# Eight experts in sequence on one core: two results instead of one go into buffers of earlier results, and both leave by SyncE and ScalarE

## The chip, the cores and the metric

The kernel runs on one core of one Trainium2 chip. The metric is the device time of one execution in microseconds (us). Four executions of the kernel before gave 183.13, 183.03, 182.60 and 182.73 us, a median of 182.88 us. Lower is better.

## The reference: what is computed

Eight experts each apply a two-layer network to their own 256 rows of input. All inputs and outputs are float32.

```python
n_experts, capacity, hidden, expert_hidden = 8, 256, 512, 2048
h = np.matmul(x, w1) + b1[:, np.newaxis, :]      # (8,256,512) @ (8,512,2048)
h = np.maximum(h, 0)
return (np.matmul(h, w2) + b2[:, np.newaxis, :]).astype(np.float32)   # @ (8,2048,512)
```

Each expert has 4 MB of `w1` and 4 MB of `w2`, 512 KB of `x` and 512 KB of result. The profile counts 71.39 MB read from device memory and 4.19 MB written to it.

## The kernel before, in words

The weights are read once, as float32, and turned into float16 on the way by DMAs that GpSimd issues. Everything that GpSimd issues, loads and stores, is written by hand into one list, called `ring` (lines 214 to 225), and stays in that order (`ordered`). The main loop (lines 227 to 234) has stages s = 0 to 10. A stage first puts out the entries of the ring that are due, then computes the first product of expert s (`first_product`: 64 matrix multiplications into PSUM, and ReLU with bias on ScalarE) and the second product of expert s - 3 (`second_product`: the bias row and 32 matrix multiplications into two PSUM tiles `po0` and `po1`). The lag of three stages is `LAG`.

The entries of the ring are, in order, the loads of x, w1 and w2, the second weights of expert 7 in three pieces (8, 4 and 4 sixteenths; `load_w2_piece`), and after all loads the stores: `flush(0)`, `flush(1)` and so on, `flush(e)` being due in stage e + 4 (line 225). So the stores of results 0 to 3 are put out in stage 7, right behind the last load, and those of results 4, 5 and 6 in stages 8, 9 and 10.

GpSimd's DMAs use eight completion semaphores in turn. A DMA is therefore issued only when the one eight places before it has landed. This paces the stores: in the trace each `out_dram<-out` issue on POOL ends a wait for the landing of a piece of weights.

`store(e, po)` (lines 139 to 154) brings a result from PSUM to SBUF: VectorE copies the half `po[0]` (L145), ScalarE the half `po[1]` (L146). The result tile is 128 partitions of 4 KB; partition p holds rows 2p and 2p + 1. For results 0 to 6 the tile comes from `out_pool`, which has seven buffers. Two of the seven first hold the float32 x of experts 0 and 1 (`x32`) and become results 5 and 6. Result 7 has no buffer of its own: it is written into that of result 4 (`REUSED = 4`), so its copies must wait until the store of result 4 has landed. Its store is issued by SyncE (L149).

Result 5 is stored in three pieces (`PARTS`, line 37): partitions 0 to 24 by SyncE as soon as the copies are done (L153), partitions 25 to 120 and 121 to 127 by GpSimd when `flush(5)` is due (L137). All other stores are whole, by GpSimd. In what follows, store e is the store of result e.

Of the kernel before, what the change touches and what calls it, by code (L numbers as in the profile page):

```python
# [11 lines left out]
def kernel(  # L12
# [9 lines left out]
    nc = tc.nc  # L22
    fp32 = mybir.dt.float32
    fp16 = mybir.dt.float16
    E, T, H = x.shape
    M = w1.shape[2]
    P = 128
# [1 line left out]
    nKC = H // P  # L29
    nJ = M // P  # L30
    LAG = 3
    LATE = range(E - 1)
    REUSED = 4

    PARTS = {5: ((0, 25, True), (25, 121, False), (121, 128, False))}
    nXF32 = 2

    def ordered(ins):  # L40
        return tc.keep_in_program_order(ins)
# [5 lines left out]
    x_pool = ctx.enter_context(tc.tile_pool(name="xp", bufs=4))  # L47
    xT_pool = ctx.enter_context(tc.tile_pool(name="xTp", bufs=2))
    hT_pool = ctx.enter_context(tc.tile_pool(name="hT", bufs=LAG + 1))
    out_pool = ctx.enter_context(tc.tile_pool(name="outp", bufs=E - 1))  # L50
    psum_x = ctx.enter_context(tc.tile_pool(name="psum_x", bufs=1, space=bass.MemoryType.PSUM))
    psum_h = ctx.enter_context(tc.tile_pool(name="psum_h", bufs=3, space=bass.MemoryType.PSUM))
    psum_o = ctx.enter_context(tc.tile_pool(name="psum_o", bufs=2, space=bass.MemoryType.PSUM))
# [13 lines left out]
    results = []  # L67
    pending = {}
# [63 lines left out]

    def flush(e):
        dst, src = pending.pop(e)
        for p0, p1, sync in PARTS.get(e, ((0, P, False),)):
            if not sync:
                ordered(nc.gpsimd.dma_start(out=dst[p0:p1], in_=src[p0:p1]))  # L137

    def store(e, po):


        if e < E - 1:
            results.append(out_pool.tile([P, nTB, H], fp32, tag="out", name="out"))
        out_sb = results[e] if e < E - 1 else results[REUSED]
        nc.vector.tensor_copy(out=out_sb[:, 0, :], in_=po[0])  # L145
        nc.scalar.copy(out=out_sb[:, 1, :], in_=po[1])  # L146
        dst = out[e].rearrange("(p tb) h -> p tb h", tb=nTB)
        if e == E - 1:
            nc.sync.dma_start(out=dst, in_=out_sb)  # L149
            return  # L150
        for p0, p1, sync in PARTS.get(e, ()):
            if sync:
                nc.sync.dma_start(out=dst[p0:p1], in_=out_sb[p0:p1])  # L153
        pending[e] = (dst, out_sb)

    def second_product(e):
        po = []
        for tb in range(nTB):
            t = psum_o.tile([P, H], fp32, tag=f"po{tb}", name=f"po{tb}")
            po.append(t)  # L160
            ordered(nc.tensor.matmul(  # L161
                out=t, lhsT=ones1, rhs=b2_sb[0:1, e * H : (e + 1) * H], start=True, stop=False,
            ))
        for lo, hi, t in w2_sb[e]:
            for tb in range(nTB):
                for j in range(lo, hi):
                    ordered(nc.tensor.matmul(  # L167
                        out=po[tb],
                        lhsT=hT[e][:, j, tb * P : (tb + 1) * P],
                        rhs=t[:, j - lo, :],  # L170
                        start=False,
                        stop=(j == nJ - 1),
                    ))
        store(e, po)

    x32 = []
    for e in range(nXF32):
        x32.append(out_pool.tile([P, nTB, H], fp32, tag="out", name="x32"))
        (nc.sync if e == 0 else nc.scalar).dma_start(
            out=x32[e], max_dma_last_dim=2048, in_=x[e].rearrange("(p tb) h -> p tb h", tb=nTB)  # L180
# [4 lines left out]
        out=b2_sb,  # L185
        in_=b2.rearrange("e h -> (e h)").rearrange("(o f) -> o f", o=1),
# [10 lines left out]
    for j in range(nJ):  # L197
        for s in range(2):
            ordered(nc.tensor.matmul(  # L199
                out=pb[s * 64 : (s + 1) * 64, j, :, :],  # L200
# [5 lines left out]
    for s in range(2):  # L206
        nc.vector.tensor_copy(  # L207
            out=b1T[s * 64 : (s + 1) * 64, :, :], in_=pb[s * 64 : (s + 1) * 64, :, :, s]
# [13 lines left out]
    for lo, hi in ((0, 8), (8, 12), (12, 16)):  # L222
        ring.append((0, load_w2_piece, (E - 1, lo, hi)))
    for e in LATE:
        ring.append((e + LAG + 1, flush, (e,)))
# [40 lines left out]
```

## Time and profile before

| what | value | where it is from |
|---|---|---|
| median of four executions | 182.88 us | the times |
| the profiled execution's own time | 183.13 us | the times |
| its span in the trace | 181.3 us | the page |
| outside the span | 1.8 us | 183.13 - 181.3 |
| granted TensorE clock, mean | 0.924 | the times |
| TensorE busy | 135.2 us, 75% | the page, part 1 |
| software DMA queue (GpSimd's) | 38.71 MB, 96.9% of 16 engines' span | the page, part 3 |
| SyncE's queue | 1.15 MB, 1.7% | the page, part 3 |
| ScalarE's queue | 0.59 MB, 1.1% | the page, part 3 |
| stores by GpSimd, 512 KB | 6, median 21.1 us from issue to landing | the page, part 6 |
| store 7 by SyncE, 512 KB | 3.2 us from issue to landing | the DMA view |

The bytes of the queues are counted as they are written, so a weight that arrives as float32 and is kept as float16 counts half. The line of DMA shares in the page gives the mean busy share of the 16 DMA engines in 40 slices of 4.5 us; a 9 means 90% or more. The share in a window can come out a little above 1, since packets of one engine overlap at their ends. In a line of the timeline the bracket gives the idle time of that engine before the instruction and what ended it.

### The profile page before, as it was taken

The numbers are of one execution on the slowest core, as the hardware profiler recorded it, in microseconds if no ns is written. First come the engines' busy times: TensorE is split into PE (matmuls) and PEld (weight loads), VectorE is DVE, ScalarE is ACT, GpSimd is POOL, SyncE is SP. The second block draws the span as 40 slices with busy tenths as digits, with TensorE's granted clock in tenths as the row PEclk, the third lists the DMA queues.
The fourth block names the chain that finished last, engine by engine and source line by source line (L and its number), as shares of the span: only waits on it lengthen the run. The fifth ranks groups of instructions, "written<-read, shape, count | busy, mean of one in ns | idle before, by whom it ended". The sixth has DMA issues, their size and how long they took to land.

```text
span 181.3 us, 2122 instructions
## 1 busy us (share of the span) xinstructions
PE 135.2 (75%) x912; PEld 94.3 (52%) x912; DVE 13.1 (7%) x21; ACT 62.5 (34%) x137; POOL 20.1 (11%) x43
## 2 busy tenths in 40 slices
PE   1725989579650999939990899939998999988900
PEld 1614879459550754936480664936497434333300
DVE  0320011001000101010100101010100101010010
ACT  0021769638670340825081250726078010101010
POOL 7200020300300010201010000200050111111200
PEclk9999999969995589999999589999999999999975
DMA  5999999999999999899989999999999999999994
GB/s 159 264 228 233 220 184 232 194 229 213 233 228 184 224 231 228 181 227 231 224 181 227 232 213 195 231 228 210 199 231 201 211 222 208 224 220 209 358 412 192
DMA packets 5543, 40.58 MB, mean 224 GB/s; under 512 B 638, under 2 KB 654, under 8 KB 3230
## 3 DMA queue, kind: packets, MB, share of 16 engines
q0 software_dynamic: 4784, 38.71, 96.9%
q1 hardware_dynamic: 446, 1.15, 1.7%
q10 hardware_dynamic: 304, 0.59, 1.1%
q8 instruction: 7, 0.11, 0.2%
q14 instruction: 2, 0.02, 0.0%
HBM read 71.39 MB, written 4.19 MB: 417 GB/s over the span
## 4 chain that ended last, share of the span: by engine, by line
DMA 75%; PE 19%; issue 1%; POOL 1%; DVE 0%; POOLq 0%; DVEq 0%
DMA x<-in_x_dram 44%; DMA w2sb<-in_w_dram 15%; PE ph L116 10%; DMA out_dram<-out 9%; DMA w1sb<-in_w_dram 8%; PE po L167 8%; PE psx L103 1%; POOL w2sb L88 1%; PE po L161 1%; DVE out L145 0%; POOL w1sb L78 0%; DVEq L145 0%; POOLq L137 0%; POOLq L250 0%
## 5 line engine op out<-in xcount | busy, mean ns | idle before, releaser
L116 PE MATMUL ph<-xT,w1sb 128*128 128x256 f16 x512 | 67.0, 296 | 10.9 <-DMA w1sb<-in_w_dram 10.9
L123 ACT ACTIVATE hT<-ph,b1T 128x256 f16<-128x256 f32 x128 | 56.9, 473 | 42.0 <-PE ph L116 41.9
L116 PEld LDWEIGHTS <-w1sb 128*128 128x128 f16 x512 | 60.8, 148 | 16.4 <-DMA w1sb<-in_w_dram 11.9
L167 PE MATMUL po<-w2sb,hT 128*128 128x512 f16 x224 | 49.7, 379 | 1.3 <-DMA w2sb<-in_w_dram 1.3
L167 PEld LDWEIGHTS <-hT 128*128 128x128 f16 x256 | 24.5, 98 | 34.0 <-issue 5.8
L146 ACT COPY out<-po 128x512 f32<-128x512 f32 x8 | 4.7, 591 | 62.9 <-PE po L167 50.8
L103 PE MATMUL psx<-ident,x 128*128 128x128 f16 x64 | 6.2, 254 | 19.7 <-DMA x<-in_x_dram 17.9
L103 PEld LDWEIGHTS <-x 128*128 128x128 f16 x64 | 5.0, 124 | 20.7 <-DMA x<-in_x_dram 18.9
L78 POOL DMA_DIRECT2D w1sb<-in_w_dram x8 | 4.5, 558 | 65.2 <-PE ph L116 64.3
L109 DVE COPY xT<-psx 128x1024 f16<-128x1024 f16 x8 | 5.5, 691 | 81.8 <-PE psx L103 81.8
L145 DVE COPY out<-po 128x512 f32<-128x512 f32 x8 | 5.5, 692 | 74.7 <-PE po L167 61.1
L88 POOL DMA_DIRECT2D w2sb<-in_w_dram x9 | 4.8, 535 | 53.7 <-PE po L167 53.7
L137 POOL DMA_DIRECT2D out_dram<-out x8 | 4.3, 532 | 31.3 <-DMA w2sb<-in_w_dram 23.0
L167 PE MATMUL po<-w,hT 128*128 128x512 f16 x32 | 7.1, 379 | 0.8 <-DMA w<-in_w_dram 0.8
L199 PE MATMUL pb<-ident,b_rows 16*64 16x16 f32 x64 | 3.7, 266 | 4.1 <-DMA b_rows<-in_b_dram 4.1
L199 PEld LDWEIGHTS pb<-ident,b_rows 16*64 16x64 f32 x64 | 3.6, 198 | 4.0 <-POOL ident masks.py:199 4.0
L161 PE MATMUL po<-b_sb,ones 1*128 1x512 f16 x16 | 4.8, 379 | 0.0
L123 ACT ACT_TABLE_LOAD x1 | 1.3, 1283 | 9.5 <-DVE b1T L207 9.5
L72 POOL DMA_DIRECT2D x<-in_x_dram x6 | 3.6, 604 | 0.5 <-DMA w1sb<-in_w_dram 0.5
L161 PEld LDWEIGHTS <-ones 1*128 1x128 f16 x16 | 0.9, 92 | 2.1 <-issue 2.1
L194 DVE CAST x<-x 128x1024 f16<-128x1024 f32 x2 | 1.4, 694 | 6.6 <-DMA x<-in_x_dram 6.6
L94 POOL DMA_DIRECT2D w<-in_w_dram x3 | 1.6, 557 | 0.0
(9 smaller groups left out, 2.6 us busy)
## 6 DMA issues: line engine op xcount, KB each, us to landing
w1sb<-in_w_dram POOLq DMA_DIRECT2D x8, 2048.0 KB, 33.8
w2sb<-in_w_dram POOLq DMA_DIRECT2D x5, 2048.0 KB, 46.4
w2sb<-in_w_dram POOLq DMA_DIRECT2D x4, 1024.0 KB, 28.7
out_dram<-out POOLq DMA_DIRECT2D x6, 512.0 KB, 21.1
x<-in_x_dram POOLq DMA_DIRECT2D x6, 256.0 KB, 39.2
w<-in_w_dram POOLq DMA_DIRECT2D x1, 1024.0 KB, 31.1
w<-in_w_dram POOLq DMA_DIRECT2D x2, 512.0 KB, 34.1
x<-in_x_dram SPq DMA_DIRECT2D x1, 512.0 KB, 4.2
```

Of the source, the lines that this page charges most:

```text
L78: ordered(nc.gpsimd.dma_start(out=w1_sb[e], in_=w1[e].rearrange("(p kc) m -> p kc m", kc=nKC)))
L88: ordered(nc.gpsimd.dma_start(out=t[:, lo : lo + step, :], in_=src[:, lo : lo + step, :]))
L103: ordered(nc.tensor.transpose(out=pt[:, kc, tb * P : (tb + 1) * P], in_=x16[e][:, tb, :].rearrange("p (q kc) -> p q kc", kc=nKC)[:, :, kc] ...
L109: nc.vector.tensor_copy(out=xT[e], in_=pt)
L116: ordered(nc.tensor.matmul(out=ph, lhsT=w1_sb[e][:, kc, :].rearrange("p (q j) -> p q j", j=nJ)[:, :, j], rhs=xT[e][:, kc, :], start=(kc == 0),
L123: nc.scalar.activation(out=hT[e][:, j, :], in_=ph, func=mybir.ActivationFunctionType.Relu, bias=b1T[:, j, e : e + 1], scale=1.0,)
L137: ordered(nc.gpsimd.dma_start(out=dst[p0:p1], in_=src[p0:p1]))
L145: nc.vector.tensor_copy(out=out_sb[:, 0, :], in_=po[0])
L146: nc.scalar.copy(out=out_sb[:, 1, :], in_=po[1])
L161: ordered(nc.tensor.matmul(out=t, lhsT=ones1, rhs=b2_sb[0:1, e * H : (e + 1) * H], start=True, stop=False,))
L167: ordered(nc.tensor.matmul(out=po[tb], lhsT=hT[e][:, j, tb * P : (tb + 1) * P], rhs=t[:, j - lo, :], start=False, stop=(j == nJ - 1),))
L199: ordered(nc.tensor.matmul(out=pb[s * 64 : (s + 1) * 64, j, :, :], lhsT=b1_rows.rearrange("r (q j) -> r q j", j=nJ)[:, :, j], rhs=ident[0 ...
```

## The change

Result 6 no longer has a buffer of its own: it is written into the buffer of result 2, and result 7 into that of result 3 instead of result 4. The pool has six buffers instead of seven; results 4 and 5 now take the two that first held x32. GpSimd stores results 0 to 5, each whole, in the ring; results 6 and 7 are stored outside the ring, at once after their copies. Store 7 is whole, by SyncE. Store 6 is cut as store 5 was: partitions 0 to 24 by SyncE, 25 to 120 by ScalarE, 121 to 127 by SyncE.

```diff
-    LATE = range(E - 1)
-    REUSED = 4
-    PARTS = {5: ((0, 25, True), (25, 121, False), (121, 128, False))}
+    REUSED = {E - 2: 2, E - 1: 3}
+    LATE = range(E - 2)
+    PARTS = {E - 2: ((0, 25, False), (25, 121, True), (121, 128, False))}
...
-    out_pool = ctx.enter_context(tc.tile_pool(name="outp", bufs=E - 1))
+    out_pool = ctx.enter_context(tc.tile_pool(name="outp", bufs=E - 2))
...
     def flush(e):
         dst, src = pending.pop(e)
-        for p0, p1, sync in PARTS.get(e, ((0, P, False),)):
-            if not sync:
-                ordered(nc.gpsimd.dma_start(out=dst[p0:p1], in_=src[p0:p1]))
+        ordered(nc.gpsimd.dma_start(out=dst, in_=src))
...
     def store(e, po):
-        if e < E - 1:
+        if e in REUSED:
+            out_sb = results[REUSED[e]]
+        else:
             results.append(out_pool.tile([P, nTB, H], fp32, tag="out", name="out"))
-        out_sb = results[e] if e < E - 1 else results[REUSED]
+            out_sb = results[e]
         nc.vector.tensor_copy(out=out_sb[:, 0, :], in_=po[0])
         nc.scalar.copy(out=out_sb[:, 1, :], in_=po[1])
         dst = out[e].rearrange("(p tb) h -> p tb h", tb=nTB)
-        if e == E - 1:
-            nc.sync.dma_start(out=dst, in_=out_sb)
+        if e in LATE:
+            pending[e] = (dst, out_sb)
             return
-        for p0, p1, sync in PARTS.get(e, ()):
-            if sync:
-                nc.sync.dma_start(out=dst[p0:p1], in_=out_sb[p0:p1])
-        pending[e] = (dst, out_sb)
+        for p0, p1, scalar in PARTS.get(e, ((0, P, False),)):
+            (nc.scalar if scalar else nc.sync).dma_start(out=dst[p0:p1], in_=out_sb[p0:p1])
```

## The prediction

> **What bounds the kernel now.** I read the page's slices and queues first, then the last 15 us: chain, timeline, windows. The first lines are the slices of TensorE and of the DMA engines, the bytes moved, and the queues.
>
> ```profile
> PE   1725989579650999939990899939998999988900
> DMA  5999999999999999899989999999999999999994
> GB/s 159 264 228 233 220 184 232 194 229 213 233 228 184 224 231 228 181 227 231 224 181 227 232 213 195 231 228 210 199 231 201 211 222 208 224 220 209 358 412 192
> q0 software_dynamic: 4784, 38.71, 96.9%
> ```
>
> The DMA engines are full from start to end and TensorE is idle in the last two slices. So the time is the work of the DMA engines, plus any time that the last of them stands idle. In slices 38 and 39 only stores run: 412 GB/s. Now the chain of the end, in order of time, with its columns start, length and what, and the timeline of the instructions that the change touches.
>
> ```profile
> 133.31 26.70 DMA w2sb<-in_w_dram
> ...
> 160.59 15.64 DMA out_dram<-out
> 176.23 0.03 issue
> 176.26 0.05 DVEq L145
> 176.31 0.04 issue
> 176.35 0.69 DVE out L145
> ```
>
> ```profile
> 155.85 0.35 SPq L153 DMA_DIRECT2D out_dram<-out  x1
> ...
> 161.98 0.69 DVE L145 COPY out<-po 128x512 f32<-128x512 f32 x1 [7.78 <-PE po L167]
> ...
> 163.71 0.58 ACT L146 COPY out<-po 128x512 f32<-128x512 f32 x1 [7.88 <-PE po L167]
> ...
> 165.01 7.07 PE L167 MATMUL po<-w,hT 128*128 128x512 f16 x32 [0.80 <-DMA w<-in_w_dram]
> ...
> 165.55 0.52 POOL L137 DMA_DIRECT2D out_dram<-out  x1 [4.43 <-DMA w<-in_w_dram]
> 167.72 0.52 POOL L137 DMA_DIRECT2D out_dram<-out  x1 [1.65 <-DMA w<-in_w_dram]
> 170.47 0.55 POOL L137 DMA_DIRECT2D out_dram<-out  x1 [2.22 <-DMA w<-in_w_dram]
> 176.33 0.58 ACT L146 COPY out<-po 128x512 f32<-128x512 f32 x1 [12.04 <-DMA out_dram<-out]
> 176.35 0.69 DVE L145 COPY out<-po 128x512 f32<-128x512 f32 x1 [13.68 <-DMA out_dram<-out]
> 177.12 0.35 SPq L149 DMA_DIRECT2D out_dram<-out  x1
> ```
>
> TensorE ends at 172.1, but the copies of result 7 wait until 176.3 for store 4 to land. It looks like a 4.2 us loss. The windows say whether it is one:
>
> ```profile
> 174.00:176.00 2.00, 0.00 (x0) 0.00 (x0) 0.00 (x0) 0.00 (x0) 0.00 (x0) 0.53 1.02 408
> 176.00:178.00 2.00, 0.00 (x0) 0.00 (x0) 0.69 (x1) 0.58 (x1) 0.00 (x0) 0.50 0.84 334
> 178.00:180.00 2.00, 0.00 (x0) 0.00 (x0) 0.00 (x0) 0.00 (x0) 0.00 (x0) 0.50 0.65 264
> ```
>
> The last two columns are DMA share and GB/s. The engines were full until 176 with the stores before; only afterwards is some of them idle, 0.16 x 2 us on the mean, and the 0.65 holds the end itself.
>
> Whether that idle time lies on the engines that end last is read from the trace's records of DMA packets and completion increments (each DMA engine adds one to a store's semaphore when its share has landed). Store 4: four engines at 175.00 to 175.08, twelve at 175.73 to 176.23. Store 6: four at 177.21 to 177.61, eleven at 178.05 to 178.53, one at 179.09. Store 7: fifteen at 179.57 to 179.76, one at 180.34. A store's packet is one partition, 4 KB; eight per engine make up a whole store, and whole stores land 1.24 us apart: 0.155 us a packet. For the later of the regular engines store 7 lands 1.23 us after store 6 (178.53 to 179.76): no idle time there. The idle time is that of the four early engines (177.2 to the first packet of store 7 at 177.97). The single late one had one packet of 0.74 us at 176.11, a stall of 0.58 us. The span ends 1.0 us after the last landing.
>
> **The change, part by part.** The sum is made against the profiled execution: 183.13 us, span 181.3, 1.8 outside; it is 0.25 above the median of 182.88.
>
> *Store 5 whole, by GpSimd.* Its SyncE piece (25 packets of 0.17 us, 159.21 to 163.1, five increments: five packets on each of five engines) leaves the time of the loads. Before it, nine engines finished a piece of weights at 158.8 to 159.0 and the others up to 160.02; after it only four were early. So it went to five early engines and the landing that TensorE waits for (164.97) was not theirs: 0 gained. If that cover weren't there, it would be 5 x 0.17 = 0.85. GpSimd issues six stores, not eight: 2 x 0.53 us less on an engine that is idle. Store 5's issue waits for the landing at 164.97 as now.
>
> *Copies of result 6.* They move from 161.98 and 163.71 to behind store 2, whose last increment is at 173.73: 173.8 to 174.5. Behind them on VectorE and ScalarE stand only the copies of result 7. TensorE needs none of it, as `po` has two buffers and expert 7 uses the other. This delay of 12 and 10 us costs nothing as long as the DMA engines hold other stores: stores 3, 4 and 5 keep them busy until 176.2 (early ones) to 177.4.
>
> *Three issues for store 6.* SyncE 0.35 (row of L149) from 174.55, ScalarE about 0.46 (its two issues at the start took 0.45 and 0.47), SyncE 0.35 more, until 175.3. ScalarE's next is its copy of result 7, which waits until 175.1 anyway. First packets follow the issue by 0.85 us if the engines' queues are short (177.12 to 177.97) and by 3.36 behind weight packets of 0.6 us (155.85 to 159.21): between 175.4 and 177.9. The queue ahead is of 0.155 us packets, so I take 176.0, near the short end.
>
> *Store 7.* Its copies wait for store 3 (last increment 175.06), not store 4 (176.23): 1.17 us earlier, 175.15 to 175.85. SyncE issues at 175.95, its two pieces of store 6 being out; first packets at 176.8 instead of 177.97.
>
> *What the engines carry.* Behind store 4 the five engines of the unequal deal, now early at about 175.0, carry 8 (store 5) + 5 + 6 + 1 (store 6) + 8 (store 7) = 28 packets: 175.05 + 28 x 0.155 = 179.4. Seven late engines carry 22 or 23: 176.23 + 3.41 or 3.57 = 179.64 or 179.80. The four early ones end at 178.5. Before, the last regular increment was 179.76. So the work of the engines that end last is the same: -0.1 to +0.05, and with the stall unchanged 0. The gain of 1.17 us in store 7's start goes to engines that were going to end first.
>
> *The stall.* If it falls on a moment when a second queue has packets, part of it may be hidden: 0 to -0.58. One run in two or so shows it, by the times (183.13 and 183.03 against 182.60 and 182.73). *The tail.* SyncE's closing waits cost 0.06 us each where satisfied; several stores now land together: 0 to +0.3.
>
> Sum against 183.13: 0 + 0 - 0.05 - 0.3 + 0.1, or 182.9; against the median, where the stall weighs half, -0.05 - 0.25 + 0.1 = -0.2, or 182.65 with rounding. That is no change that can be measured: a measurement of this kernel tells about 0.2%, 0.37 us, from no change.
>
> *A rule against the row.* Store 5 in the trace of before is a case of a cut store: its 28 KB piece lands 0.16 to 0.22 us behind its 384 KB piece, on every engine, and hides in the stream, so I charge the two cuts nothing beyond their packets. The Trainium skill, in "DMA: Bandwidth & Descriptors", section "Rules for kernel authors", advises against cutting a transfer by partitions, as the parts use the same engines, and its fit in "Anatomy of one DMA" has about 2.0 us of fixed cost for each DMA; an estimate by that page, with two more DMAs in series, would be some 4 us more, 186.7.
>
> **The rivals.**
>
> *Faster, 182.3.* The several queues fill the gaps: no engine stands idle at a change from one store to the next and the stall is hidden. Behind store 4 the last regular engine took 176.23 to 179.76, 3.53 us for 22 or 23 packets (3.41 or 3.57), so 0.1; with the stall 0.58 and half a weight, -0.4, and up to -0.6. For it: 0.84 in the window from 176. Against it: that idle time is on the early engines.
>
> *Slower, 184.1.* SyncE's and ScalarE's packets start as late as the piece of store 5 did. Five engines then stand empty between the end of store 5's share (175.05 + 1.24 = 176.3) and 177.9, and after it have 20 packets of 0.155: 177.9 + 3.1 + 0.3 to land = 181.3, against 179.76 or, with the stall, 180.34: +1.0 to +1.5, +1.2 on the median. It decides from a start at about 176.4, when 20 packets no longer end before 179.8. Against it: 0.85 at store 7, with queues of small packets. If the first five engines are not the early ones in every execution, the price is 176.23 + 28 x 0.155 = 180.6, +0.8 or 183.7, on the same side.
>
> *Same, for another reason.* The copies of results 6 and 7 are so late that the earlier start is lost again, but the engines still hold stores 4 and 5: 182.9.
>
> **How the numbers follow.** No measurable change, in either form, 0.46, at 182.65, own range 182.5 to 183.25. Faster by over 0.2% 0.32: the stall and the gaps can give that, if most of it comes. Slower 0.22. The range leaves out about 0.07 below 182.2 and 0.13 above 183.45.
>
> **What would show it.** Right: the copies of result 6 begin near 173.8 and those of result 7 near 175.2; both waits are for `out_dram<-out`; SyncE's last issue is near 176; the window from 176 to 178 has a share near 1; the last landing is still near 179.7. Wrong: a share under 0.9 from 175 to 178, first packets of store 6 after 176.4, store 2 or 3 landing later than now, or increments of store 7 that end at 179.2 or before.

## The result and the profile after

The changed kernel takes 183.03 us (median of 48 runs), the kernel before 182.66 us (median of 72). The ratio is 1.0019, with a 95% interval of 1.0015 to 1.0024: slower by 0.37 us, just under the 0.2% that the forecast took as no change, and clear of one by the interval. The median of before is lower than the 182.88 shown before the prediction, because two of those four, 183.13 and 183.03, are among the only 7 of the 72 above 183.0; the trace of the 183.13 one has one engine that ends late.

The profiled execution of the changed kernel took 183.14 us, span 181.4, 1.8 outside. Its timeline at the end, with the same columns as that of before:

```profile
173.74 0.58 ACT L146 COPY out<-po 128x512 f32<-128x512 f32 x1 [16.95 <-DMA out_dram<-out]
173.76 0.69 DVE L145 COPY out<-po 128x512 f32<-128x512 f32 x1 [18.59 <-DMA out_dram<-out]
174.54 0.35 ACTq L152 DMA_DIRECT2D out_dram<-out  x1
174.54 1.58 SPq L152 DMA_DIRECT2D out_dram<-out  x3
174.98 0.59 ACT L146 COPY out<-po 128x512 f32<-128x512 f32 x1 [0.66 <-DMA out_dram<-out]
175.00 0.69 DVE L145 COPY out<-po 128x512 f32<-128x512 f32 x1 [0.55 <-DMA out_dram<-out]
```

The moves came out as forecast: the copies of result 6 start at 173.74, those of result 7 at 174.98, and SyncE is done issuing at 176.12 instead of 177.47. The windows of the changed kernel (last columns clock, DMA share, GB/s):

```profile
174.00:176.00 2.00, 0.00 (x0) 0.00 (x0) 1.14 (x2) 0.91 (x2) 0.00 (x0) 1.00 1.02 418
176.00:178.00 2.00, 0.00 (x0) 0.00 (x0) 0.00 (x0) 0.00 (x0) 0.00 (x0) 0.73 1.01 395
178.00:180.00 2.00, 0.00 (x0) 0.00 (x0) 0.00 (x0) 0.00 (x0) 0.00 (x0) 0.50 0.46 186
```

The idle time from 176 to 178 is gone (share 1.01, 0.84 before), and the engines are emptier after 178 (0.46, 0.65 before). By the completion increments, the last store lands at 179.95; in the profile of before it was 180.34, with one stalled engine, and 179.76 without it. So the stores are not what became slower in this pair of profiles: the last landing is 0.39 us earlier and the span is as long. (Against 179.76 it is 0.19 later; in the profiles without a stalled engine further down, stores of either kernel land at 179.80 to 179.84.) The time went behind the last landing: 1.41 us to the end of the span, 1.01 before.

What stands there is the closing sequence: SyncE waits for all stores and reports to GpSimd, GpSimd signals the other engines, drains, clears the semaphores and signals again. It shows in the waits of SyncE's queue (line, whom it waited for, us in total, times, longest). The kernel before, then the changed one:

```profile
SPq L261 <- PEq L261: 0.8, 2, 0.5
```

```profile
SPq L259 <- PEq L259: 1.2, 2, 1.0
```

The second of its two waits at the barrier takes 1.0 us instead of 0.5. (The profile puts it down to TensorE's queue, which sends the last of the signals; the engine that it is waiting for is GpSimd.) The view of the closing line, GpSimd's drains (ns min/median/max, first and last start us), before and after:

```profile
L261 POOLq DRAIN  x3: 46/98/9770, 170.8 to 181.1; - x3
```

```profile
L259 POOLq DRAIN  x3: 40/250/13278, 165.5 to 181.1; - x3
```

A drain is an instruction in which the engine waits for work of its own. The longest is the one behind GpSimd's last DMA: in the changed kernel it ends at 178.77, 1.40 us behind the last landing of a store of GpSimd. The middle value is the second drain, in the closing sequence: 250 ns instead of 98. In the instructions of the trace it also starts late: GpSimd's signal ends at 180.22 and the drain starts at 180.64, 0.42 us later; before, 180.71 and 180.78, 0.07.

At about the same place an instruction packet appears (queue and kind, packets, MB, share). The DMA queues of the kernel before between 173.5 and 174.5, and of the changed kernel between 180.5 and 182:

```profile
q14 instruction: 1, 0.01, 1.9%
```

```profile
q14 instruction: 1, 0.01, 2.1%
```

It is one packet of 8 KB in each, at 173.98 before and at 181.36 after; the rest of the closing window is empty. Counting GpSimd's instructions that the trace records, in order of time and from 0, number 68 is the drain behind the last DMA in the kernel before, and the drain in the closing sequence in the changed one, which has three records fewer (73 instead of 76: two DMA issues and one semaphore wait). In both kernels number 68 starts late: before, 0.33 us after the DMA ahead of it (170.47, 170.80), where the same drain in the changed kernel starts together with that DMA (165.51, 165.49). That gave the theory that was tested: **GpSimd asks for its next 8 KB of code at a fixed place in its instruction list, is held for about 0.4 us there, and the change moved that place into the closing sequence**. The rival was that stores 6 and 7 end later by the way they are dealt and issued.

### The profile page after: what moved, and what is told of

Same layout as the page of the kernel before. It is cut to its first block, busy times and chain, and to the rows that moved or that the text cites. A ratio compares the mean times of both kernels' runs of the same rounds, so it can differ in the third digit from the quotient of the medians.

```text
span 181.4 us, 2125 instructions
## 1 busy us (share of the span) xinstructions
PE 135.7 (75%) x912; PEld 94.4 (52%) x912; DVE 13.1 (7%) x21; ACT 62.5 (34%) x137; POOL 19.1 (11%) x41
## 4 chain that ended last, share of the span: by engine, by line
DMA 63%; PE 31%; issue 1%; POOL 1%; DVE 1%; DVEq 0%; POOLq 0%
DMA x<-in_x_dram 44%; PE po L165 15%; PE ph L118 14%; DMA out_dram<-out 11%; DMA w1sb<-in_w_dram 8%; PE po L159 1%; PE psx L105 1%; DVE out L145 1%; POOL w2sb L90 0%; POOL w1sb L80 0%; DVEq L145 0%; POOLq L248 0%; POOLq L137 0%
## 5 line engine op out<-in xcount | busy, mean ns | idle before, releaser
L137 POOL DMA_DIRECT2D out_dram<-out x6 | 3.2, 533 | 25.8 <-DMA w2sb<-in_w_dram 9.4
```

## The experiments

All ratios are to the kernel before, timed on the same chip beside it; its median there was 182.69 to 182.76. A ratio need not be the quotient of the two medians; it differs from it by up to 0.001, so single ratios are read with their intervals.

**The code load moved forward: four memsets.** Added to the changed kernel, behind the last GpSimd store:

```diff
+    scrap = singles.tile([1, 16], fp32)
...
+        if s == E + LAG - 1:
+            for i in range(4):
+                ordered(nc.gpsimd.memset(scrap[:, i : i + 1], 0.0))
```

> The changed kernel with four one-element memsets on GpSimd behind its last store; nothing else differs. Code theory: in the changed kernel GpSimd's 68th recorded instruction is the DRAIN in the closing sequence, it starts 0.42 us late (180.22 to 180.64), and the 8 KB instruction packet that answers it comes at 181.36; in the kernel before the 68th is the DRAIN behind the last DMA, 0.35 us late at 170.8, with the packet at 173.98, where nobody waits. With four instructions more the load falls before the closing sequence: 183.03 - 0.4 = 182.6, ratio to the kernel before 0.998 to 1.000, an 8 KB packet before 179, and 1.0 us from the last landing to the end of the span instead of 1.4. DMA theory (stores 6 and 7 end later because of how they are dealt): no change, 183.0, ratio 1.0015 to 1.0024, the 1.4 us may shrink but the last landing is then later than 179.95.

Measured: 182.62 us, ratio 0.9997 (0.9986 to 1.0008). The four added instructions make the kernel some 0.4 us faster. The instruction packet is at 169.32, the last landing at 179.80, and 0.93 us lie behind it. Its waits of SyncE:

```profile
SPq L263 <- PEq L263: 0.7, 2, 0.5
```

**The loss made in the kernel before, with its stores untouched.**

```diff
-    make_identity(nc, ident16)
+    nc.vector.tensor_copy(out=ident16, in_=ident)
```

> The kernel before with three GpSimd instructions fewer at the start: the float16 identity is copied from the float32 one by VectorE. The stores are those of before. Code theory: the load of GpSimd's code moves three instructions later, into the closing sequence, as in the changed kernel: 182.66 + 0.35 = 183.0, ratio 1.0015 to 1.0025, the 8 KB packet after 180, 1.4 us from the last landing to the end. DMA theory: the same as before, ratio 0.9995 to 1.0005, since the stores are untouched.

Measured: 183.11 us, ratio 1.0019 (1.0008 to 1.0030). Three GpSimd instructions fewer, some 178 us before the end, cost as much as the whole change. The last landing is at 179.84, the end 1.5 us later. The waits of SyncE and GpSimd's drains, as in the changed kernel:

```profile
SPq L261 <- PEq L261: 1.3, 2, 1.0
```

```profile
L261 POOLq DRAIN  x3: 40/243/9542, 170.5 to 181.1; - x3
```

and the instruction packet is at 181.37. This is the run that the rival can't explain.

**Two controls.** The four memsets in the kernel before, and both edits together.

> The kernel before with the four memsets behind its last store, a control for the cost of the memsets. Both theories: 182.66, ratio 0.9995 to 1.0005; the code is loaded a few instructions earlier, where GpSimd has nothing urgent.

> The kernel before with the float16 identity copied by VectorE (three GpSimd instructions fewer, as in the run that took 183.11) and the four memsets behind the last store. Code theory: the memsets bring the code load forward again, and the time is that of the kernel before, ratio 0.9990 to 1.0005. If the copy of the identity by VectorE was itself the cost: 183.0 to 183.1, ratio 1.0015 to 1.0025.

Measured: 182.61 us, ratio 1.0003 (0.9990 to 1.0015), and 182.67 us, ratio 1.0004 (0.9992 to 1.0016). The memsets cost nothing, and they take away what the missing identity had cost; the copy by VectorE is not the cause.

**One memset or two.** The same edit of the changed kernel with `range(1)` and `range(2)`.

> The changed kernel with one memset on GpSimd behind its last store. Code theory, by place: GpSimd's 68th recorded instruction in program order is now the signal that it sends between SyncE's report and the second DRAIN; the 0.4 us still lies in the closing sequence, so 183.0 us, ratio 1.0015 to 1.0025, 1.4 us from the last landing to the end. If instead the memsets help because GpSimd is kept busy longer, or because of where they put its DRAIN, one memset helps as four did: 182.6, ratio 0.9990 to 1.0005.

> The changed kernel with two memsets. Code theory, by place: the 68th is now the instruction that waits for SyncE's report; it is fetched while GpSimd would wait anyway (its first DRAIN ends near 178.8, SyncE reports near 180), so the 0.4 us is hidden: 182.6, ratio 0.9990 to 1.0005, 1.0 us from the last landing to the end. If the gain came in small steps with each memset, this would be near 182.8.

Measured: with one 182.93 us, ratio 1.0013 (1.0004 to 1.0022), a little under the expected 1.0015; with two 182.50 us, ratio 0.9993 (0.9984 to 1.0001). One instruction more decides over 0.4 us. The closing line with one memset, from 179.5 on, then with two:

```profile
L263 POOLq EVENT_SEMAPHORE  x4: 17/17/17, 180.0 to 181.1; - x4
L263 POOLq DRAIN  x2: 51/110/170, 180.5 to 180.9; - x2
```

```profile
L263 POOLq EVENT_SEMAPHORE  x4: 17/17/17, 180.0 to 180.7; - x4
L263 POOLq DRAIN  x2: 51/78/105, 180.2 to 180.5; - x2
```

With one, GpSimd takes SyncE's report at 179.99 and signals at 180.44, and the drain follows at once (180.52): the gap has moved exactly one instruction forward. With two, it lies before the instruction that waits for the report, and nothing of it is seen: 180.01, 180.09, 180.18. The instruction packets are at 181.13 and 179.81. The table has the closing sequence of all of them, in us of each span, from the instructions of the trace.

| kernel | last landing | GpSimd takes the report | signals | second drain | behind the last landing | 8 KB packet |
|---|---|---|---|---|---|---|
| before | 180.34 | 180.61 | 180.70 | 180.78 to 180.88 | 1.01 | 173.98 |
| changed | 179.95 | 180.12 | 180.21 | 180.64 to 180.89 | 1.41 | 181.36 |
| before, three fewer | 179.84 | 180.12 | 180.20 | 180.64 to 180.88 | 1.50 | 181.37 |
| changed, one memset | 179.81 | 179.99 | 180.44 | 180.52 to 180.69 | 1.36 | 181.13 |
| changed, two | 179.84 | 180.01 | 180.09 | 180.18 to 180.28 | 0.92 | 179.81 |
| changed, four | 179.80 | 179.97 | 180.05 | 180.13 to 180.24 | 0.93 | 169.32 |

**What the stores are worth by themselves.** Three kernels: the kernel before with `REUSED = 3`; the kernel before with four memsets and store 5 whole (`PARTS = {}`); the changed kernel with four memsets and store 6 whole by ScalarE (`PARTS = {E - 2: ((0, P, True),)}`).

> The kernel before with result 7 in the buffer of result 3 instead of result 4, GpSimd's list unchanged. It tells what store 7's earlier start is worth alone. Forecast's step: its copies begin 1.2 us earlier, at 175.1, its packets near 176.8, and the engines that end last have no idle time to fill: 182.6 to 182.7, ratio 0.9990 to 1.0005. If the idle time after 176 sets the end: up to 0.5 us less, 182.2, ratio 0.997.

> The kernel before with store 5 whole by GpSimd, and the four memsets so that GpSimd's code is loaded early in any case. It tells what the unequal deal of store 5 is worth. If the late DMA engines set the end: they carry 24 packets behind store 4 instead of 22 or 23, +0.16 to +0.31 us, 182.8 to 182.95, ratio 1.0009 to 1.0017. If the deal is worth nothing, as the run of the changed kernel with store 6 whole suggests: ratio 0.9990 to 1.0005.

> The changed kernel with the four memsets, and store 6 whole by ScalarE (eight packets on each DMA engine) in place of the three unequal pieces. It tells what the unequal deal is worth, beside the run with the memsets alone. If the deal sets the end: the seven late engines carry 24 packets behind store 4 instead of 22 or 23: 176.12 + 24 x 0.155 + the landing = 179.8 to 180.0 instead of about 179.5 to 179.7, +0.2 to +0.35 us, ratio 1.001 to 1.002 with the code loaded early. If the deal is worth nothing (DMA engines not the bound at the end): the same time as the run with the memsets alone.

Measured: 182.62 us, ratio 0.9994 (0.9983 to 1.0005); 182.55 us, ratio 0.9993 (0.9984 to 1.0001); 182.54 us, ratio 0.9989 (0.9980 to 0.9997). With the buffer of result 3, store 7 is issued at 176.23 instead of 177.12 and the window from 176 is full, and nothing is won. The issue and the windows of that kernel, in an execution of 183.38 us in which one engine ends late (180.54, the others by 179.83):

```profile
176.23 0.35 SPq L149 DMA_DIRECT2D out_dram<-out  x1
```

```profile
176.00:178.00 2.00, 0.00 (x0) 0.00 (x0) 0.15 (x1) 0.03 (x1) 0.00 (x0) 0.50 0.99 395
178.00:180.00 2.00, 0.00 (x0) 0.00 (x0) 0.00 (x0) 0.00 (x0) 0.00 (x0) 0.50 0.48 195
```

The unequal deal wins nothing either; if it set the end, whole stores were to cost 0.16 to 0.35 us. With store 6 whole and four memsets the last increments are nine at 178.54 to 179.04 and seven at 179.68 to 179.84: the late engines carry 24 packets and end at 179.84, where the dealt version ends too (179.80 to 179.95). By count the deal takes one or two packets from the late engines and gives four to five others. Which engines end last with it is not shown, since the increments don't name their engine; packets slowed as told below are one candidate for the lost saving. By its interval the version with store 6 whole is faster than the kernel before, by 0.11%; whether that is a shorter usual time or the lack of late runs (its highest is 182.60 us, that of the kernel before 183.40) is not told apart.

**The slow packets.** In the profiles of both kernels some 4 KB packets at the start of a cut store take 0.3 to 0.74 us. The changed kernel with four memsets and store 6 cut at a multiple of 32:

```diff
-    PARTS = {E - 2: ((0, 25, False), (25, 121, True), (121, 128, False))}
+    PARTS = {E - 2: ((0, 32, False), (32, 128, True))}
```

> The changed kernel with the four memsets and store 6 cut evenly: partitions 0 to 31 by SyncE (two packets on each engine), 32 to 127 by ScalarE (six). In the traces with a store cut at 25 and 121, single 4 KB packets of 0.3 to 0.7 us stand at the start of its pieces and the times reach 183.4 to 183.5; with whole stores there are none and the times stay within 0.14 us. If the cut as such brings them, they are here too and the spread of the times is over 0.3 us. If the unequal shares or the borders at 25 and 121 do, there are none over 0.3 us and the times stay within 0.2 us. Median in both cases 182.5 to 182.65, ratio 0.9985 to 1.0002.

Measured: 182.55 us, ratio 0.9993 (0.9984 to 1.0002). Slow packets are there (eleven of 0.3 to 0.56 us), but all times lie within 0.25 us. The expectation is half missed: the cut as such brings slow packets, yet they don't make a late run here. In the executions that were profiled at 183.1 to 183.4 (the kernel before, the kernel before with four memsets, and with the buffer of result 3) one engine ends 0.6 to 0.7 us behind the others. In 34 runs with whole stores or the even cut no time was above 182.70; in the 72 of the kernel before, seven were above 183.0. Against a simple rule: the kernel before with three instructions fewer has the same cut, no slow packet in its profile (none above 0.18 us) and a spread of 0.27 us, so the expectation's "in the traces with a store cut at 25 and 121" did not hold for all of them. What makes one engine late stays open.

## Why the prediction was right or wrong

The forecast of 182.65 us, no measurable change, was low by 0.38. It had the time 0.2 us under the median of the four executions, and the kernel came out 0.37 us over the median of before. That the range held the time is luck: its upper part stood for a late start of the stores' pieces, which did not come.

**Right: the engines that end last keep their work.** "The gain of 1.17 us in store 7's start goes to engines that were going to end first" is what the runs show: with the code load out of the way the changed kernel is at 0.9993 and 0.9997, and the earlier buffer alone at 0.9994, all with 1 in the interval. The copies, issues and first packets (175.82, forecast 176.0) came where they were put. The fixed cost of a cut store was rightly left out: with four memsets, store 6 in three pieces and whole are within 0.1 us (182.62 and 182.54). The estimate by the Trainium skill, in "DMA: Bandwidth & Descriptors", section "Anatomy of one DMA", was some 4 us; the page's fit is for DMAs that GpSimd issues, and these pieces went by SyncE and ScalarE. The signs that the prediction named for being right nearly all came (copies at 173.74 and 174.98, share 1.01, the last landing at 179.95 for "near 179.7"), and none of them lies behind the last landing.

**Wrong: "GpSimd issues six stores, not eight: 2 x 0.53 us less on an engine that is idle".** The step priced the removed instructions by their duration and found them off the path. No run shows their duration to be worth anything. But removing them shifted everything behind them in GpSimd's list, and a hold of about 0.4 us at a fixed place in that list moved from behind the last DMA, where GpSimd had 9.8 us to wait, into the closing sequence, where all engines wait for it. That is +0.49 us of single profiles (1.41 against 0.92 behind the last landing, in the changed kernel and with two memsets). The forecast had put the end at "1.0 us after the last landing" and took that for constant.

**Wrong in kind: the tail.** The +0.1 for SyncE's closing waits did not come; the waits for the other stores are done by 178.79, before the last landing. Instead 0.09 us was gained: with store 6 on GpSimd, its first drain ends later (180.57) than SyncE reports (180.48), as it ends 1.4 to 1.5 us behind the last landing of GpSimd's own stores (179.09 before; 177.37 and 178.77 after). With its last store earlier, this is off the path (1.01 before, 0.92 in the changed kernel with two memsets).

**Wrong in size: the stall.** I gave it half a weight from four runs, -0.25. Times above 183.0, of which the trace of 183.13 shows it, are 7 of 72, so the median holds next to none of it. Without the stall, +0.49 - 0.09 is +0.40, against 0.37 measured.

**Slips in the working that decide nothing.** In the trace of before the last increment of store 2 is at 173.66 and that of store 3 at 175.14, where the prediction has 173.73 and 175.06; by these store 7's copies were due 1.09 us earlier, not 1.17 (they came 1.35 earlier). ScalarE's issue took 0.35 us, not 0.46. The term of the engines' work was worked out as 0 and entered as -0.05, and 182.88 - 0.2 is 182.68, not 182.65.

**Rivals.** Neither the late start of SyncE's and ScalarE's pieces nor the filled gaps decided: first packets came 1.3 us behind the issue, and the slower side, which had 0.22, was reached by a mechanism that was not among the rivals.

**What stays inferred.** That the count of GpSimd's instructions places the hold is shown, by one instruction. That the hold is the request for code, and the 8 KB packet its answer, is an inference from their order: the packet has no engine's name, but it follows the hold in each of the traces (0.7 us behind its end in the three kernels that have it in the closing sequence, 3.1 to 3.4 us when the queues are full, and with two memsets, where the hold isn't seen, 1.1 us behind the end of the first drain), and no other engine's list was changed in the runs with memsets. The Trainium skill, in "Runtime: NRT & Kernel Launch", section "Instruction fetch mechanics", describes such a fetch: a sequencer loads its next block of instructions over a DMA queue of its own while it runs the current one, and crossing a block is mostly hidden. The page's block is 16 KiB; the packet here is 8 KB. If the hold is this fetch, the runs agree with the first, as GpSimd goes on 0.7 us before the packet comes, and show where the second fails: 0.49 us in the closing sequence.

## What to carry to other kernels

An instruction removed from an idle engine is not free of consequence: here it put other instructions at the place in that engine's list where it is held for about 0.4 us, taken above for the load of its code. At this scale (0.2%), compare the time behind the last landing in both profiles before blaming the transfers, and look for an instruction packet in the last few us; two to four instructions of padding on the engine that runs the closing sequence tell in one run (one was not enough here). And idle time in a mean DMA share, as the run with the buffer of result 3 shows, is worth filling only if it lies on the engines that end last.

## What the runs showed of the hardware that was not expected

- A hold of about 0.4 us on GpSimd at a fixed place of its list: 0.42 us plus a drain longer by 0.15 in the changed kernel, 0.44 between report and signal with one memset, none seen with two.
- GpSimd's drain ends 1.4 to 1.5 us behind the last landing of its own DMAs (1.48 in the kernel before, 1.40 in the changed one), so a last store by GpSimd reaches further into the closing sequence than one by SyncE.
- Single 4 KB packets of 0.3 to 0.74 us instead of 0.155 at the start of cut stores in eight of the ten profiles that have one, and none above 0.25 us in the other two (both with the float16 identity copied by VectorE) and in the two profiles with whole stores.
